# Quarter sums moved from GpSimd to VectorE, seven products added up in PSUM on copied seeds, first gate group left whole

## The chip, the cores and the metric

One core of one Trainium2 chip runs the whole program. The metric is the device time of one execution in microseconds (us). The kernel before takes 1243.79 us, the median of three runs (1243.25 to 1244.95).

Engines are named as the profile names them: PE is TensorE (PEld its weight loads), DVE is VectorE, ACT is ScalarE, POOL is GpSimd, SP is SyncE, which issues nearly all DMAs.

## The reference

Two transformer blocks follow each other on 512 tokens of width 1024, all in float32. The change touches the second block's feed-forward part alone:

```python
D_FF = -(-8 * D_MODEL // (3 * 256)) * 256          # 2816
h = rmsnorm_2(x, ffn_norm_g[l])
x = x + (jax.nn.silu(h @ w_gate[l]) * (h @ w_up[l])) @ w_down[l]
return rmsnorm_2(x, final_norm_g)
```

Here h is 512 x 1024 and w_gate and w_up are 1024 x 2816.

## The kernel before

Each float32 operand of a matmul is split in two float32r parts, high (`hi`, `wh`) and low (`lo`, `wl`), and each product is three matmuls: high by high, high by low, low by high. For a weight tile, ACT casts the high part (line 257) and DVE subtracts it to get the low part (line 258). Four weight tiles (`wh`, `wl`) are held at a time; `used` (L261) frees one when PE has finished it, and converts the next one that fits.

**Gate and up in seven products.** Columns of w_gate and w_up are taken in 12 groups (`quartered`): group 0 is gate columns 0 to 511, group 1 is up columns 0 to 511, and so on; groups 10 and 11 are 256 wide. A group's weight is cut into four quarters (A11, A21, A12, A22: two halves of the 1024 rows by two halves of the columns), and so is h (B11, B21, B12, B22: two halves of the width by two halves of the tokens). With the sums S1 to S4 of weight quarters and T1 to T4 of quarters of h, seven quarter products replace eight (the Winograd form of Strassen's scheme). `SEVEN` (L158) names, for each product, the operand of h, the PSUM bank R1 to R4 that it goes to, and whether it starts that bank afresh (`True`) or adds to what is there.

Each quarter product of a full group is 24 matmuls (2 column blocks x 4 row blocks x 3) of 128 x 128 weights and 256 tokens; a group is 168 of them, groups 10 and 11 are 84 each, together 1848.

**Who does what.** `Quarters.load` (L172) brings a quarter in by DMA (512 KB) into a ring of six places; `Quarters.add` (L185) forms S1 to S4 on POOL, tile name `qsum`, in one of three places. `quarters_T` (L210), called for each block `tb` of 128 tokens, transposes the normalized activations on PE (L1214), copies them to `h3f`, splits B11 and B21 for the first two blocks, and for the last two forms T1 to T4 on POOL (L1223 to L1229, tile `tsum`), each split on ACT and DVE as soon as it is there. `Sevenfold.run` (L1293) issues the matmuls (L1301) and combines: after A11, ACT copies R1 to SBUF as p1; DVE forms u2 = p1 + R2, u3 = p1 + R2 (a second R2), and the three result quarters c22, c21, c12 (L1290); C11 is read from R1. `out` (L1273) applies silu to gate groups (tile `ag`) or multiplies up groups by it (tile `fa`).

**Order.** The list `seven` sets the order of products: A11 and A12 of groups 0 and 1 first, which need only the first 256 tokens, then the other five products of group 0, those of group 1, and from group 2 on the order of `SEVEN`. PE runs inside `ordered()` in the order written. The other engines' queues are laid out by a scheduler; each engine takes its queue strictly in order. Before this stage PE runs the out-projection's second half, `product("o21", ...)`, whose evacuation `ev_o2` (L1233) gives the normalized tokens; behind it comes the down projection (`dn0`, `dn1`, matmuls on L342), whose activations `fs` are split by `place` (L1346).

## Time and profile before

| | before |
|---|---|
| median of 3 runs | 1243.79 us |
| profiled execution: time | 1242.61 us |
| profiled execution: span | 1240.9 us |
| mean granted TensorE clock | 0.993 |
| PE, DVE, ACT, POOL busy | 96%, 70%, 49%, 24% |
| gate/up stage (first to last L1301 matmul) | 859.49 to 1110.95 us |

The time holds 1.7 us outside the span. A PE row's duration is the latency of one pipelined matmul (a 256-column one lasts 0.28 us), so PE's busy sum says little on how tight its work is packed; how far apart matmuls start, and the waits put down to PE, say more. DVE, ACT and POOL rows start a little before the one ahead of them has ended, so a queue's pace is read from start to start.

### The profile page before, as it was taken

What the parts mean: (1) busy time and instruction counts of PE and PEld (TensorE: products, weight loads), DVE (VectorE), ACT (ScalarE), POOL (GpSimd) and SP (SyncE); (2) the same over time, 40 slices, a digit from 0 to 9 for tenths busy, and PEclk for the clock granted to TensorE, in tenths of its full rate; (3) what the DMA queues carried; (4) which work ended last, traced back from release to release, by engine and by line L of the source; (5) the groups of instructions that cost most, each with busy time, mean ns of one, the idle gap of its engine ahead of it and who ended that gap; (6) DMA issues with size and microseconds to landing.
All of it is one profiled execution on the core that took longest, in us unless ns stands there. A gap on an engine that the chain in (4) does not pass through costs nothing.

```text
span 1240.9 us, 18922 instructions
## 1 busy us (share of the span) xinstructions
PE 1190.3 (96%) x6852; PEld 1031.4 (83%) x6852; DVE 868.6 (70%) x1779; ACT 603.9 (49%) x1259; POOL 296.0 (24%) x363
## 2 busy tenths in 40 slices
PE   6999999999999999899999999998699999999997
PEld 5898788888888888699888898786699999988885
DVE  5678767896677455875555788765999999985322
ACT  4565456545653344444566677535334434463212
POOL 2011033101210023402111122103855555410201
PEclk9999999999999999999999999999899999999999
DMA  5412311321123432334221312452233333244321
GB/s 188 106 58 68 121 33 53 109 83 51 52 89 119 170 119 86 119 91 112 69 68 53 88 37 68 137 170 85 67 103 104 102 112 93 69 152 122 100 86 68
DMA packets 79804, 117.19 MB, mean 94 GB/s; under 512 B 10336, under 2 KB 43360, under 8 KB 79712
## 3 DMA queue, kind: packets, MB, share of 16 engines
q1 hardware_dynamic: 79712, 115.99, 29.9%
q8 instruction: 54, 0.88, 0.3%
q14 instruction: 38, 0.31, 0.1%
HBM read 109.68 MB, written 6.29 MB: 93 GB/s over the span
## 4 chain that ended last, share of the span: by engine, by line
PE 81%; DVE 10%; issue 3%; ACT 2%; POOL 2%; DMA 1%; SPq 0%; POOLq 0%; DVEq 0%; ACTq 0%
PE mm L342 55%; PE mm L1301 11%; PE R L1301 4%; DVE wl L258 3%; PE AV L589 3%; PE T L574 2%; DVE acts L442 1%; ACT wh L257 1%; PE S L807 1%; PE S L808 1%; PE T L473 1%; DMA raw<-in_w_in_dram 1%; PE T L1100 1%; POOL var L458 0%; POOL eg L973 0%
## 5 line engine op out<-in xcount | busy, mean ns | idle before, releaser
L258 DVE TENSOR_TENSOR wl<-raw,wh 128x512 fp32r<-128x512 f32 (+6 forms) x199 | 181.2, 930 | 137.7 <-ACT wh L257 136.9
L257 ACT CAST wh<-raw 128x512 fp32r<-128x512 f32 (+6 forms) x199 | 153.9, 799 | 191.0 <-PE mm L342 126.8
L534 POOL TENSOR_SCALAR P<-P,rr 128x256 f32<-128x256 f32 (+3 forms) x128 | 69.1, 540 | 310.3 <-DVE rr L532 216.2
L1301 PE MATMUL mm<-acts,wh 128*128 128x256 f32 x704 | 128.6, 284 | 8.5 <-DVE u L1290 5.3
L1301 PEld LDWEIGHTS mm<-acts,wh 128*128 128x128 f32 x704 | 109.1, 190 | 10.3 <-issue 10.1
L342 PE MATMUL mm<-wh,fs 128*128 128x512 f32 x352 | 110.5, 395 | 0.2 <-ACT fs L444 0.2
L342 PE MATMUL mm<-hh,wh 128*128 128x512 f32 x256 | 103.6, 405 | 0.0
L342 PE MATMUL mm<-hl,wh 128*128 128x512 f32 x256 | 101.4, 396 | 0.0
L342 PE MATMUL mm<-hh,wl 128*128 128x512 f32 x256 | 100.3, 395 | 0.0
L1301 PE MATMUL mm<-acts,wl 128*128 128x256 f32 x352 | 99.4, 283 | 0.0
L442 DVE TENSOR_TENSOR pl<-T,ph 128x128 fp32r<-128x128 f32 (+3 forms) x152 | 62.3, 411 | 30.6 <-ACT ph L441 30.0
L258 DVE TENSOR_TENSOR wl<-qsum,wh 128x1024 fp32r<-128x1024 f32 (+1 forms) x48 | 81.0, 1687 | 2.6 <-ACT wh L257 2.3
L257 ACT CAST wh<-qsum 128x1024 fp32r<-128x1024 f32 (+1 forms) x48 | 46.9, 977 | 68.4 <-PE mm L1301 43.5
L342 PEld LDWEIGHTS mm<-wh,fs 128*128 128x128 f32 x352 | 65.9, 188 | 16.5 <-ACT fs L444 0.4
L1301 PE MATMUL R<-acts,wh 128*128 128x256 f32 x352 | 66.6, 289 | 13.4 <-ACT p L1307 13.4
L441 ACT CAST ph<-T 128x128 fp32r<-128x128 f32 (+3 forms) x152 | 55.1, 363 | 49.7 <-PE T L574 36.9
L192 POOL TENSOR_TENSOR qsum<-quart 128x1024 f32<-128x1024 f32 (+1 forms) x24 | 57.6, 2398 | 84.9 <-DMA quart<-in_w_gate_dram 53.6
L526 ACT ACTIVATE P<-P,nm 128x128 f32<-128x128 f32 (+2 forms) x96 | 51.5, 536 | 47.2 <-DVE nm L519 43.7
L342 PE MATMUL mm<-wl,fs 128*128 128x512 f32 x176 | 69.7, 397 | 0.4 <-DVE wl L258 0.4
L258 DVE TENSOR_TENSOR wl<-quart,wh 128x1024 fp32r<-128x1024 f32 (+1 forms) x36 | 65.6, 1828 | 4.1 <-ACT wh L257 4.1
L1301 PEld LDWEIGHTS R<-acts,wh 128*128 128x128 f32 x352 | 56.4, 196 | 13.9 <-ACT p L1307 13.8
L1301 PEld LDWEIGHTS mm<-acts,wl 128*128 128x128 f32 x352 | 67.0, 190 | 0.0
(376 smaller groups left out, 3259.6 us busy)
## 6 DMA issues: line engine op xcount, KB each, us to landing
raw<-in_w_in_dram SPq DMA_DIRECT2D x50, 512.0 KB, 3.6
raw<-in_w_down_dram SPq DMA_DIRECT2D x22, 512.0 KB, 3.7
quart<-in_w_gate_dram SPq DMA_DIRECT2D x20, 512.0 KB, 3.9
quart<-in_w_up_dram SPq DMA_DIRECT2D x20, 512.0 KB, 3.9
raw<-in_w_merge_dram SPq DMA_DIRECT2D x16, 512.0 KB, 3.6
raw<-in_w_out_dram SPq DMA_DIRECT2D x16, 512.0 KB, 3.7
raw<-in_w_ple_gate_dram SPq DMA_DIRECT2D x8, 512.0 KB, 3.7
raw<-in_w_branch_b_dram SPq DMA_DIRECT2D x4, 512.0 KB, 3.5
```

The lines of the kernel that those rows point to most:

```text
L192: nc.gpsimd.tensor_tensor(t, self.parts[a], self.parts[b], op=op)
L257: nc.scalar.copy(hi[:, js], raw[:, js])
L258: mark[0] = nc.vector.tensor_sub(lo[:, js], raw[:, js], hi[:, js].bitcast(F32)).ins
L342: nc.tensor.matmul(o, x_, m, start=kc == 0 and k == 0 and n0 == 0, stop=last and k == 2)
L441: nc.scalar.copy(hi, src)
L442: nc.vector.tensor_sub(lo, src, hi.bitcast(F32))
L473: nc.tensor.transpose(T[:, i, :], src[:, blk(c + i)], ident)
L526: nc.scalar.activation(P[:, :n], P[:, :n], AF.Exp, bias=bias, scale=-1.0, accum_out=rs)
L534: nc.gpsimd.tensor_scalar(P[:, :n], P[:, :n], rr, 1.0, op0=OP.mult, op1=OP.mult)
L574: nc.tensor.transpose(T[:, i, :], P[:, blk(i)], ident)
L589: nc.tensor.matmul(self.av[:, q0:q0 + pc.stop - pc.start], self.v(kb), m, start=pi == 0 and i == 0, stop=pi == len(plan) - 1 and i == 1)
L1301: nc.tensor.matmul(R[:, c, :], w[:, kc, cs], m[:, kc, :], start=first and c + kc + k == 0, stop=kc == 3 and k == 2, skip_group_check=True)
```

## The change

Six things change. (1) S1 to S4 are formed on DVE, not on POOL. (2) T1 to T4 are formed on DVE, most of them later, in `quarter_sums`, called when the first gate columns are evacuated; T4 changes its sign. (3) Group 0 is no quartered group any more: `fg0` is a plain product of 512 columns by 8 row blocks, in the order "half" (first the first 256 tokens of all four column blocks, then the last 256): 192 matmuls of 256 tokens instead of 168. It needs B12 split too, and takes four 512 KB weight tiles as `raw`. (4) u2 and u3 are added up by PE: ACT copies R1 into R2's bank, on which S2 and S3 add, and then R2 into R4's bank, on which A22 adds; ACT also copies R3 (p5) and R2 (u2) to SBUF. (5) R3 moves from an `mm` bank to one of the transposes' banks (E). (6) The order of products becomes A11(1), then for each group S1, S2, A12, S3, the next group's A11, A22, S4.

```diff
     }
 
 
-    SEVEN = {"A11": ("B11", 1, True), "S1": ("T1", 3, True), "S2": ("T2", 2, True), "A12": ("B21", 1, False),
-             "S3": ("T3", 2, False), "A22": ("T4", 4, True), "S4": ("B22", 3, False)}
+    SEVEN = {"A11": ("B11", 1, True), "S1": ("T1", 3, True), "S2": ("T2", 2, False), "A12": ("B21", 1, False),
+             "S3": ("T3", 2, False), "A22": ("T4", 4, False), "S4": ("B22", 3, False)}
     ring, sums = {}, []
 
     class Quarters:
...
             t = self.parts[name] = self.view(sums[i])
             a, op, b = {"S1": ("A21", OP.add, "A22"), "S2": ("S1", OP.subtract, "A11"),
                         "S3": ("A11", OP.subtract, "A21"), "S4": ("A12", OP.subtract, "S2")}[name]
-            nc.gpsimd.tensor_tensor(t, self.parts[a], self.parts[b], op=op)
+            nc.vector.tensor_tensor(t, self.parts[a], self.parts[b], op=op)
 
         def load_for(self, name):
             for q in {"S1": ("A21", "A22"), "A11": ("A11",), "A12": ("A12",)}.get(name, ()):
...
                 self.add(name)
             return self.parts[name]
 
+    specs["fg0"] = ([(w_gate_2, 0, 512, 0)], 8)
     specs_tail = {f"dn{i}": ([(w_down_2, 512 * i, 512, 0)], 22) for i in range(2)}
     quartered = []
     for i in range(6):
         for w in (w_gate_2, w_up_2):
             quartered.append(Quarters(w, 512 * i, 512 if i < 5 else 256))
-    early = ("A11", "A12")
-    seven = [(g, name) for g in (0, 1) for name in early]
-    seven += [(g, name) for g in (0, 1) for name in SEVEN if name not in early]
-    seven += [(g, name) for g in range(2, 12) for name in SEVEN]
+
+    seven = [(1, "A11")]
+    for g in range(1, 12):
+        seven += [(g, name) for name in ("S1", "S2", "A12", "S3")]
+        seven += [(g + 1, "A11")] if g < 11 else []
+        seven += [(g, name) for name in ("A22", "S4")]
 
     stream, first_of = [], {}
 
...
             else:
                 names, tag = {"B11": (("B11", "B21"), "U0"), "B21": (("B11", "B21"), "U0"),
                               "T3": (("T3", "B22"), "U1"), "B22": (("T3", "B22"), "U1"),
-                              "T1": (("T1", "T2"), "U6"), "T2": (("T1", "T2"), "U6")}[name]
-                t = unit("acts", tag, [128, 4, 4, 256])
+                              "T1": (("T1", "T2"), "U6"), "T2": (("T1", "T2"), "U6"),
+                              "B12": (("B12",), "U4")}[name]
+                t = unit("acts", tag, [128, 2 * len(names), 4, 256])
                 for i, n in enumerate(names):
                     acts[n] = [t[:, 2 * i], t[:, 2 * i + 1]]
         return acts[name]
...
             return
         b11, b21 = [h3f[:, c:c + 4, blk(tb - 2)] for c in (0, 4)]
         b12, b22 = [h3f[:, c:c + 4, blk(tb)] for c in (0, 4)]
-        t1, t2, t3, t4 = [p2("tsum", [128, 4, 128]) for _ in range(4)]
-        nc.gpsimd.tensor_sub(t1, b12, b11)
-        act_split("T1", tb, t1)
-        nc.gpsimd.tensor_sub(t2, b22, t1)
-        act_split("T2", tb, t2)
-        nc.gpsimd.tensor_sub(t3, b22, b12)
-        act_split("T3", tb, t3)
-        nc.gpsimd.tensor_sub(t4, t2, b21)
-        act_split("T4", tb, t4)
+        act_split("B12", tb, b12)
         act_split("B22", tb, b22)
+        sums_T.append((tb, b11, b12, b21, b22))
+
+    sums_T = []
+
+    def quarter_sums():
+
+        t12 = {}
+        for tb, b11, b12, b21, b22 in sums_T:
+            t12[tb] = [p2("tsum", [128, 4, 128]) for _ in range(2)]
+            nc.vector.tensor_sub(t12[tb][0], b12, b11)
+            act_split("T1", tb, t12[tb][0])
+            nc.vector.tensor_sub(t12[tb][1], b22, t12[tb][0])
+            act_split("T2", tb, t12[tb][1])
+        for tb, b11, b12, b21, b22 in sums_T:
+            t3, t4 = [p2("tsum", [128, 4, 128]) for _ in range(2)]
+            nc.vector.tensor_sub(t3, b22, b12)
+            act_split("T3", tb, t3)
+            nc.vector.tensor_sub(t4, b21, t12[tb][1])
+            act_split("T4", tb, t4)
 
     def ev_o2(nh):
         def f(tb, ps):
...
 
         def bank(self, i):
             if i not in self.R:
-                b = s_bank("R") if i == 1 else mm_bank()
+                b = s_bank("R") if i == 1 else t_bank("E").rearrange("p a b -> p (a b)") if i == 3 else mm_bank()
                 self.R[i] = b[:, :256 * self.n].rearrange("p (c t) -> p c t", c=self.n)
             return self.R[i]
 
...
                 ft, at = fa_at(4 * (self.g // 2) + c)
                 nc.vector.tensor_mul(ft[:, at:at + n, tok], v, gates[half][:, :n, tok])
 
-        def plus(self, name, a, b, op=OP.add):
-            t = self.sb(name)
-            nc.vector.tensor_tensor(t, a, b, op=op)
-            return t
-
         def run(self, name, hi, lo):
             b, i, first = SEVEN[name]
             bh, bl = act_pair(b)
...
                         nc.tensor.matmul(R[:, c, :], w[:, kc, cs], m[:, kc, :], start=first and c + kc + k == 0,
                                          stop=kc == 3 and k == 2, skip_group_check=True)
                     yield 0.5
-            s, R = self.s, self.R
+            R = self.R
             if name == "A11":
-                s["p1"] = self.sb("p1")
-                nc.scalar.copy(s["p1"], R[1])
+                nc.scalar.copy(self.bank(2), R[1])
+            elif name == "S1":
+                self.p5 = self.sb("p5")
+                nc.scalar.copy(self.p5, R[3])
             elif name == "S2":
-                s["u2"] = self.plus("u2", s["p1"], R[2])
+                self.u2 = self.sb("u2")
+                nc.scalar.copy(self.u2, R[2])
             elif name == "A12":
                 self.out(0, 0, R[1])
             elif name == "S3":
-                s["u3"] = self.plus("u3", s["p1"], R[2])
-                self.out(1, 1, self.plus("c22", s["u3"], R[3]))
+                nc.scalar.copy(self.bank(4), R[2])
+                c22 = self.sb("c22")
+                nc.vector.tensor_add(c22, R[2], self.p5)
+                self.out(1, 1, c22)
             elif name == "A22":
-                self.out(1, 0, self.plus("c21", s["u3"], R[4], OP.subtract))
+                self.out(1, 0, R[4])
             elif name == "S4":
-                self.out(0, 1, self.plus("c12", s["u2"], R[3]))
+                c12 = self.sb("c12")
+                nc.vector.tensor_add(c12, R[3], self.u2)
+                self.out(0, 1, c12)
 
     def sevenfold():
         groups = {}
...
             if g not in groups:
                 groups[g] = Sevenfold(g)
             if name == "S1" and g % 2 == 0:
-                gates.clear() if g else None
+                gates.clear()
             convert_to(i)
             for c in groups[g].run(name, *ws[i]):
                 yield c
                 tick(c)
             used(i)
 
+    class Halves:
+
+
+        def __init__(self, *halves):
+            self.halves = halves
+
+        def __getitem__(self, key):
+            return self.halves[key[1].start // 256][key[0], key[1].start % 256:(key[1].stop - 1) % 256 + 1]
+
+    def act_halves(kc):
+        h, k = divmod(kc, 4)
+        return [Halves(*[act_pair(f"B{h + 1}{t}")[i][:, k, :] for t in (1, 2)]) for i in range(2)]
+
+    def ev_g(c, ps):
+        if not gates:
+            gates.update({i: pool.tile([128, 2, 512], F32, name="ag", tag=f"V{2 + i}") for i in range(2)})
+            quarter_sums()
+        silu_gate(gates[c // 2][:, c % 2, :], ps)
+
     with ordered():
-        for _ in itertools.chain(product("o21", pair_act(yh, yl), ev_o2(1), True, "all"), sevenfold()):
+        for _ in itertools.chain(product("o21", pair_act(yh, yl), ev_o2(1), True, "all"),
+                                 product("fg0", act_halves, ev_g, False, "half"), sevenfold()):
             pass
 
     ssf = pool.tile([128, NB, 2], F32, name="ssf", tag="ssf")
```

**DVE at the start of the stage.** Before, from the evacuation of the last token block (`x_8945<-x_8945,mm` is its residual sum) on; `wl<-quart` are low parts of quarters, `acts` low parts of B and T:

```order
L1236 TENSOR_TENSOR x_8945<-x_8945,mm 128x512
L258 TENSOR_TENSOR wl<-quart,wh 128x1024 x3
L442 TENSOR_TENSOR acts<-tsum,acts 128x4x128
L1243 SCALAR_TENSOR_TENSOR xn<-x_8945,rstd,gb 128x1024
L258 TENSOR_TENSOR wl<-qsum,wh 128x1024
L442 TENSOR_TENSOR acts<-h3f,acts 128x4x128
L442 TENSOR_TENSOR acts<-tsum,acts 128x4x128 x2
L442 TENSOR_TENSOR t_9314<-tsum,t_9313 128x4x128
```

After, the same place; `wl<-raw` are the low parts of fg0's weight tiles 1 to 3, `tsum` T sums, `qsum` S sums:

```order
L1251 TENSOR_TENSOR x_8945<-x_8945,mm 128x512
L261 TENSOR_TENSOR wl<-raw,wh 128x1024
L1237 TENSOR_TENSOR tsum<-h3f 128x512
L1239 TENSOR_TENSOR tsum<-h3f,tsum 128x512
L1258 SCALAR_TENSOR_TENSOR xn<-x_8945,rstd,gb 128x1024
L445 TENSOR_TENSOR acts<-h3f,acts 128x4x128
L261 TENSOR_TENSOR wl<-raw,wh 128x1024
L192 TENSOR_TENSOR qsum<-qsum,quart 128x1024
L445 TENSOR_TENSOR acts<-tsum,acts 128x4x128
L445 TENSOR_TENSOR acts<-h3f,acts 128x4x128
L445 TENSOR_TENSOR acts<-tsum,acts 128x4x128
L261 TENSOR_TENSOR wl<-raw,wh 128x1024
```

DVE now forms four sums here itself, and fg0's tiles 2 and 3 (the last two `wl<-raw`) stand behind them.

**DVE over one full up group.** Before, group 3: `u` and `c` are the sums on L1290:

```order
L1290 TENSOR_TENSOR u_10124<-p_10063,mm 128x512
L258 TENSOR_TENSOR wl<-qsum,wh 128x1024
L1286 TENSOR_TENSOR fa<-R,ag 128x2x256
L258 TENSOR_TENSOR wl<-quart,wh 128x1024
L1290 TENSOR_TENSOR u_10187<-p_10063,mm 128x512
L1290 TENSOR_TENSOR c_10189<-u_10187,mm 128x512
L258 TENSOR_TENSOR wl<-qsum,wh 128x1024
L1286 TENSOR_TENSOR fa<-c_10189,ag 128x2x256
L1290 TENSOR_TENSOR c_10222<-u_10187,mm 128x512
L258 TENSOR_TENSOR wl<-qsum,wh 128x1024
L1286 TENSOR_TENSOR fa<-c_10222,ag 128x2x256
L1290 TENSOR_TENSOR c_10255<-u_10124,mm 128x512
```

After, group 3 (`c` are c22 and c12, E is R3's bank):

```order
L1301 TENSOR_TENSOR fa<-R,ag 128x2x256
L261 TENSOR_TENSOR wl<-qsum,wh 128x1024
L192 TENSOR_TENSOR qsum<-quart 128x1024
L261 TENSOR_TENSOR wl<-qsum,wh 128x1024
L1328 TENSOR_TENSOR c_10191<-mm,p_10097 128x512
L192 TENSOR_TENSOR qsum<-quart,qsum 128x1024
L1301 TENSOR_TENSOR fa<-c_10191,ag 128x2x256
L261 TENSOR_TENSOR wl<-qsum,wh 128x1024
L1301 TENSOR_TENSOR fa<-mm,ag 128x2x256
L192 TENSOR_TENSOR qsum<-quart 128x1024
L261 TENSOR_TENSOR wl<-quart,wh 128x1024
L1334 TENSOR_TENSOR c_10285<-E,u_10127 128x512
```

Per group two u sums and c21 have gone, and four `qsum` have come, each some products ahead of its use.

**ACT over one full up group.** Before, group 3, from p1's copy (`p_10063<-R`) to the next group's:

```order
L1307 COPY p_10063<-R 128x512
L257 CAST wh<-quart 128x1024
L257 CAST wh<-qsum 128x1024
L257 CAST wh<-quart 128x1024
L257 CAST wh<-qsum 128x1024 x2
L257 CAST wh<-quart 128x1024
L257 CAST wh<-qsum 128x1024
L1307 COPY p_10287<-R 128x512
```

After, group 3: `p` is R3's copy p5, `u` is u2, `mm<-mm` the seed of R4, `mm<-R` the seed of R2 for the next group:

```order
L1319 COPY p_10097<-E 128x512
L260 CAST wh<-quart 128x1024
L1322 COPY u_10127<-mm 128x512
L260 CAST wh<-qsum 128x1024 x2
L1326 COPY mm<-mm 128x512
L260 CAST wh<-qsum 128x1024
L1316 COPY mm<-R 128x512
L260 CAST wh<-quart 128x1024
```

Between the casts of weights (7 a group, as before) stand four copies out of PSUM instead of one.

## Rows read from the trace of the kernel before

**Rows 1.** Page: busy us (share), instructions by engine.

```profile
PE 1190.3 (96%) x6852; PEld 1031.4 (83%) x6852; DVE 868.6 (70%) x1779; ACT 603.9 (49%) x1259; POOL 296.0 (24%) x363
```

**Rows 2.** Windows: us; busy of PE, PEld, DVE, ACT, POOL; PEclk, DMA.

```profile
859.49:915.00 55.51, 38.35 (x281) 37.35 (x279) 53.57 (x37) 25.39 (x35) 41.54 (x19) 0.88 0.25 76
915.00:1080.00 165.00, 160.92 (x1349) 159.86 (x1349) 158.85 (x130) 71.02 (x81) 87.26 (x33) 1.00 0.32 96
1080.00:1110.95 30.95, 29.54 (x242) 28.63 (x241) 26.21 (x44) 16.36 (x30) 7.33 (x6) 1.00 0.42 142
1110.95:1240.90 129.95, 122.41 (x526) 98.11 (x524) 45.37 (x53) 36.70 (x54) 11.25 (x16) 0.98 0.30 96
```

**Rows 3.** Waits of PE, 850 to 1115 us: total, times, longest.

```profile
PE R L1301 <- ACT p L1307: 13.4, 2, 8.6
PE mm L1301 <- DVE u L1290: 5.3, 2, 2.9
```

**Rows 4.** PE in time: start, us, instruction, [idle before <-releaser].

```profile
868.59 0.80 PE L1301 MATMUL R<-acts,wh 128*128 128x256 f32 x2 [4.82 <-ACT p L1307]
...
885.26 0.79 PE L1301 MATMUL R<-acts,wh 128*128 128x256 f32 x2 [8.56 <-ACT p L1307]
...
898.34 0.48 PE L1301 MATMUL mm<-acts,wh 128*128 128x256 f32 x2 [2.89 <-DVE u L1290]
```

**Rows 5.** Chain that ended last, in time: start, us, what.

```profile
1006.55 2.84 PE R L1301 x24
1009.39 5.69 PE mm L1301 x48
...
1018.93 3.27 DVE wl L258
```

**Rows 6.** DVE groups by shape, 915 to 1080 us: busy, mean ns, idle.

```profile
L258 DVE TENSOR_TENSOR wl<-qsum,wh 128x1024 fp32r<-128x1024 f32 x33 | 61.2, 1855 | 2.0 <-ACT wh L257 1.9
L258 DVE TENSOR_TENSOR wl<-quart,wh 128x1024 fp32r<-128x1024 f32 x24 | 50.3, 2098 | 2.2 <-ACT wh L257 2.2
```

**Rows 7.** POOL groups by shape, 915 to 1080 us.

```profile
L192 POOL TENSOR_TENSOR qsum<-quart 128x1024 f32<-128x1024 f32 x15 | 38.5, 2570 | 19.5 <-DVE wl L258 19.5
```

**Rows 8.** DVE in time, around the start of the stage.

```profile
860.49 0.68 DVE L1236 TENSOR_TENSOR x<-x,mm 128x512 f32<-128x512 f32 x1
...
896.39 1.22 DVE L258 TENSOR_TENSOR wl<-qsum,wh 128x1024 fp32r<-128x1024 f32 x1
897.52 0.68 DVE L1290 TENSOR_TENSOR u<-p,mm 128x512 f32<-128x512 f32 x1
898.12 3.06 DVE L258 TENSOR_TENSOR wl<-qsum,wh 128x1024 fp32r<-128x1024 f32 x1
```

**Rows 9.** POOL in time, around the start of the stage.

```profile
864.68 1.41 POOL L451 TENSOR_TENSOR rstd<-var,mhalf 128x1 f32<-128x1 f32 x1
...
897.68 2.41 POOL L192 TENSOR_TENSOR qsum<-quart 128x1024 f32<-128x1024 f32 x1 [4.10 <-DVE wl L258]
```

**Rows 10.** DVE groups by shape, 1111 to 1150 us (POOL idle).

```profile
L258 DVE TENSOR_TENSOR wl<-raw,wh 128x1024 fp32r<-128x1024 f32 x9 | 11.0, 1222 | 13.7 <-ACT wh L257 13.7
L445 DVE SCALAR_TENSOR_TENSOR fs<-fa,fs 128x512 fp32r<-128x512 f32 x16 | 10.0, 682 | 0.0
```

**Rows 11.** ACT groups by shape, 915 to 1080 us.

```profile
L257 ACT CAST wh<-qsum 128x1024 fp32r<-128x1024 f32 x32 | 33.5, 1048 | 44.5 <-PE mm L1301 28.6 <-PE R L1301 7.3 <-issue 4.0
L1307 ACT COPY p<-R 128x512 f32<-128x512 f32 x8 | 4.6, 578 | 0.0
```

**Rows 12.** ACT in time: second h copy of block 2; first fs.

```profile
862.78 0.57 ACT L1215 COPY h3f<-T 128x512 f32<-128x512 f32 x1
...
1103.88 2.19 ACT L444 ACTIVATE fs<-fa 128x512 fp32r<-128x512 f32 x4
```

**Rows 13.** DMA issues, 855 to 1110 us: KB, median us to landing.

```profile
quart<-in_w_up_dram SPq DMA_DIRECT2D x18, 512.0 KB, 3.9
```

**Rows 14.** DMA issues, 785 to 800 us; the same columns.

```profile
quart<-in_w_up_dram SPq DMA_DIRECT2D x2, 512.0 KB, 6.3
```

## The prediction

> **What bounds the kernel now.** I read the page's busy shares first, then the stretches of the gate/up stage, PE's waits in it and what PE did in time there, and last the rows of DVE and POOL. PE is busy 96% of the span [rows 1], so only work taken from PE, or holes in its work, can move the time. The windows show where the holes are: the granted clock is 1.00 from 915 us to 1110.95 us, but 0.88 in the first 55.5 us of the stage, where PE's latencies overlap to only 38.35 us [rows 2].
>
> How tight PE could be is read from the chain: 72 matmuls in 2.84 + 5.69 = 8.53 us, 0.1185 us each at full clock [rows 5]. The stage has 1848 of them, 219.0 us, and lasts 251.5 us (859.49 to 1110.95). Transposes (16 of 128 columns) and 4 down-projection matmuls of 512 columns take about 2 us, an estimate by the same time per column. So some 30.5 us of the stage are loss:
> - Middle stretch: 165 - 1349 x 0.1185 = 5.1 us.
> - Last stretch: 30.95 less 238 x 0.1185 and 0.95 for the four down matmuls: 1.8 us.
> - First stretch: the rest, 23.6 us.
>
> In the first stretch three stalls of 4.82, 8.56 and 2.89 us [rows 4] make 16.3; the remainder is mostly the clock (12% of 55.5 us is 6.7). The profile puts the two long ones on ACT's copy of p1, once 8.6 us, and the third on a u sum of DVE [rows 3]. Those are last links only: the queues in front of them are full of T and S sums on POOL and of DVE subtractions that run slowly beside them.
>
> That slowness is the second thing to see. A low-part subtraction of 128x1024 takes 1.22 us when POOL is idle [rows 10] and the same one 3.06 us while POOL adds from 897.68 on [rows 8, 9]; over the middle stretch its mean is 1.86 and 2.10 us [rows 6]. DVE is thereby busy 158.85 of 165 us [rows 2]: it sets the pace of the middle, by a little. In the chain a slow wl of 3.27 us stands where PE's products end [rows 5].
>
> **The change part by part.** *Sums leave POOL.* A POOL sum lasts 2.57 us in the mean [rows 7], and costs DVE more than DVE's own sum would: each subtraction that it overlaps loses 1 to 2 us. In start-to-start time a DVE instruction takes 1.13 us for 1024 elements and 0.60 for 512 (starts at 896.39, 897.52, 898.12) [rows 8]. A full group after: 7 low parts and 4 sums, 11 x 1.13 = 12.4 us; 2 combining sums and 4 outputs, 6 x 0.60 = 3.6; together 16.0 us. PE needs 168 x 0.1185 = 19.9 us a group. DVE before needs 20 us of its 20.6 us a group (158.85 of 165). So PE becomes the bound, with 3.9 us a group to spare on DVE. A DVE sum of two 1024-element SBUF tiles is not in the trace; its neighbours are the subtraction alone, 1.22, and beside POOL, up to 3.06 [rows 8, 10]. I take 1.22, since no POOL work is left beside it; the upper end is the slow rival. POOL's rstd, 1.41 us behind a T sum [rows 9], also gets shorter, and the last block's normalized rows come earlier.
>
> Here a rule of the Trainium skill speaks against the change. "Perfetto Trace Analysis", section "Optimizing Scalar/DVE Operations", advises moving work off a saturated DVE, to ScalarE or even GpSimd; this does the reverse, on a DVE at 96% of its stretch. By that half the sum would be that of the slow rival below. The same passage warns that the two engines share a read port, so that moving work between them may not help; by this half DVE's load falls, as I take it. The durations with and without POOL bear out the second half.
>
> *In-order waits.* Each `qsum` is about one product ahead of need or more: S1 of a group stands on DVE before the low part of the previous group's A12, some nine products (25 us) before PE uses it. Its quarter lands in a median 3.9 us [rows 13], and its ring place frees with an S3 sum about two products (5.7 us) earlier. Held behind a late one would be the low parts, three products (8.5 us) ahead of PE. So I cost these waits at nothing; without that cover each would cost its lateness, once a group.
>
> *Seeds.* S2 waits for R2's copy, some three products ahead: hidden. Two copies have just one product's time, 2.84 us [rows 5]: u2 (R2 to SBUF) before S3, hidden by A12, and R2 to R4 before A22, hidden by the next A11. Ahead of each in ACT's queue is one cast. Cast 1.05 and copy 0.58 [rows 11], with some 0.1 of signalling, make 1.75 us: 1.1 us to spare. A copy from PSUM to PSUM is not in the trace; between 0.58 (PSUM to SBUF) and 1.05 (SBUF to SBUF, double the size) it stays hidden at both ends. The u3, c21 and one u sum that go lie off PE.
>
> So the middle loses 0 to 2 us instead of 5.1; I take 1: **4.1 gained**.
>
> *First group whole.* 24 matmuls more, 2.8 us. It needs no T and no S sum. Walking DVE's new queue from 860.49 [rows 8] at its paces: residual sum to 861.1, tile 1 to 862.2. PE, which reaches tile 1 at about 861.7, stalls 0.6. Then T1; T2 waits for block 2's second copy (862.78 + 0.57) [rows 12]: 864.0; normalized rows 865.2; one half split 865.8; tile 2 866.9; an S sum 868.1; three splits 869.9; tile 3 871.0. PE has by then done 56 matmuls and both transposes, at about 868.8: a stall of 2.2 us, with two ends: none if the scheduled sums run quicker than this, and 4.8 us, the first stall of before [rows 4], if a weight tile's DMA is late. Tile 3's DMA can be issued when tile 1 is converted, 862.3, and lands by 866.2 [rows 13]; its cast is done at 867.5: hidden by DVE. After the stall the clock takes something: I take 1.0 us, between 0 and the 6.7 us that three stalls had. The second half of fg0's tokens, 40 matmuls later at 877, wants B12 and B22 of the last block, split by 874: hidden. Weight tiles come free only in fg0's last 2 us, so A11(1) is cast and split in the 2.3 us around its end, which I cost at nothing (0 to 1). The later T sums end near 881, before S1 needs them at 891.
>
> First stretch: 2.8 + 0.6 + 2.2 + 1.0 = 6.6 instead of 23.6: **17.0 gained**.
>
> *Last groups.* ACT's queue puts eight `fs` (2.19 us for four) [rows 12] and two casts ahead of the seed for the last A22, some 5.6 us behind A12(11); PE fills it with S3 (1.4 us) and 14 down matmuls (3.3): a hole of 1.0 against 1.8 before. **0.8 gained**, between -2 and 1.8.
>
> *Earlier.* One S sum now stands in DVE's queue among the last attention head's splits, and waits for a quarter that takes up to 6.3 us to land beside three others [rows 14]. I take **0.5 lost** (0 to 1.1).
>
> Sum: 4.1 + 17.0 + 0.8 - 0.5 = 21.4 us. The profiled execution took 1242.61 us (span 1240.9 and 1.7 around it); it would take 1221.2. The median of the runs is 1.2 us above it: **1222 us**.
>
> **The rivals.**
> 1. *DVE's order gives half back.* PE's slack of three low parts is eaten by a sum that waits for its quarter, or a seed comes late, about 1 us a group over ten groups: 1232 us. For: DVE and ACT are strictly in order, and two seeds have only 1.1 us to spare. Against: DVE has 3.9 us a group left, and landing has 1.8 us of cover at worst.
> 2. *The start is smooth.* No stall at tile 3 and no clock loss: 3 us better, and nothing lost in the middle: 1218 us or a little under. For: DVE's walk adds whole paces one after another. Against: tile 3 stands behind eight other instructions.
> 3. *DVE stays slow and becomes the bound.* If the wide instructions kept the middle's mean of 1.9 us without POOL, 11 x 1.9 + 3.6 = 24.5 us a group instead of 20.6, ten times: 39 slower, 18 gained at the ends: 1265 us. It decides from about (20.6 + 1.8 - 3.6) / 11 = 1.7 us per wide instruction. For: 1.9 is the mean that this stage shows. Against: in stretches without POOL every one is at 1.22 [rows 10].
> 4. *Nothing happens:* late loads or clock eat the start's gain and the middle stays as it is, 1243 us. Nothing in the profile asks for it.
>
> **How the numbers follow.** The forecast has 0.67, with a range of its own of 1217 to 1228 (stall 0 to 4.8, middle 0 to 2, ends as given). Rival 1 has 0.17, rival 2 0.10, rival 3 0.04, rival 4 0.02. The range 1214 to 1232 leaves out the slower half of rival 1, rival 3 and rival 4. Within 0.2% (2.5 us) is about what a measurement of this kernel can't tell from no change: 0.02. Slower: 0.04. Faster: 0.94.
>
> **What would show it.** Right: wide DVE instructions of the stage at 1.22 us and DVE near 80% busy in it; two groups in 39.8 us instead of 41; only one stall over 1 us before the first quartered product, at fg0's tile 3, on a DVE wl; the seed copies under 0.7 us and no PE wait put down to them but the last. Wrong: PE waits on ACT copies or on `qsum` once a group, DVE at 95%, or a granted clock under 0.95 over the stage's first 50 us. A time above 1232 us or below 1214 us would mean that a mechanism is missing here.

## The result, and the profile after

| | before | after |
|---|---|---|
| median of the runs beside each other | 1243.52 us (1243.14 to 1244.95, 4 runs) | 1223.53 us (1222.66 to 1225.47, 4 runs) |
| profiled execution: time, span | 1242.61, 1240.9 us | 1223.95, 1222.2 us |
| ratio of the times | | 0.9839, 95% interval 0.9822 to 0.9856 |
| stage, first gate/up matmul to last | 859.49 to 1110.95 us | 860.67 to 1094.5 us |

The forecast was 1222 us, the range 1214 to 1232. The stage's windows after, to be laid beside [rows 2] (us; busy time of PE, PEld, DVE, ACT, POOL; granted clock; DMA share and GB/s):

```profile
859.49:915.00 55.51, 52.66 (x423) 51.68 (x422) 48.20 (x57) 30.09 (x43) 0.74 (x2) 0.97 0.35 106
915.00:1080.00 165.00, 165.00 (x1400) 165.00 (x1399) 134.94 (x150) 86.06 (x117) 0.00 (x0) 1.00 0.30 93
```

PE latencies now cover the whole middle stretch, where they left 4.08 of 165 us open before. DVE is busy 82% of it, not 96%. In the first stretch the clock is 0.97 where it was 0.88, and 423 instructions of PE are recorded there, not 281.

The stalls that are left are two at the start and two at the end. PE in time (start, us, instruction, [idle before <-releaser]):

```profile
863.54 0.38 PE L345 MATMUL mm<-acts,wl 128*128 128x256 f32 x1 [0.49 <-DVE wl L261]
...
872.60 0.58 PE L345 MATMUL mm<-acts,wl 128*128 128x256 f32 x1 [2.22 <-DVE wl L261]
...
1087.56 0.74 PE L345 MATMUL mm<-wh,fs 128*128 128x512 f32 x2 [1.58 <-ACT fs L447]
1088.62 0.74 PE L345 MATMUL mm<-wl,fs 128*128 128x512 f32 x2 [0.33 <-DVE wl L261]
```

They take the place of [rows 4]. The first two stand where the prediction put them, at fg0's tiles 1 and 3 (0.6 and 2.2 foreseen). Between 873 and 1087 us PE is never seen to wait. Note the 0.58 us of the matmul behind the longer stall, against 0.38 behind the short one: the clock has fallen, and narrow windows behind the stall show for how long (from 876.60 to 878.60 us it is 1.00 again):

```profile
872.60:874.60 2.00, 2.00 (x9) 2.00 (x10) 2.00 (x3) 0.28 (x1) 0.00 (x0) 0.50 0.41 83
874.60:876.60 2.00, 2.00 (x14) 2.00 (x13) 2.00 (x4) 0.81 (x2) 0.00 (x0) 0.71 0.93 294
```

0.50 is the lower level (1.2 GHz). The chain of waits gives the price (start, us, what):

```profile
872.60 17.77 PE mm L345 x136
...
910.37 5.66 PE E L1311 x48
...
950.01 5.66 PE E L1311 x48
```

At the pace of [rows 5] the 136 matmuls would take 16.1 us, so 1.65 us are lost to the clock. The two rows behind it are the same two products, two groups apart: 950.01 - 910.37 = 39.64 us for two groups.

Two prices that were only bounded before are now rows of the groups by shape, 915 to 1080 us. First DVE, then ACT (busy, mean ns, idle):

```profile
L261 DVE TENSOR_TENSOR wl<-qsum,wh 128x1024 fp32r<-128x1024 f32 x30 | 36.7, 1224 | 10.9 <-ACT wh L260 10.9
...
L192 DVE TENSOR_TENSOR qsum<-quart 128x1024 f32<-128x1024 f32 x13 | 15.9, 1220 | 0.1
```

```profile
L1326 ACT COPY mm<-mm 128x512 f32<-128x512 f32 x8 | 4.6, 578 | 0.0
L1319 ACT COPY p<-E 128x512 f32<-128x512 f32 x8 | 4.6, 578 | 0.0
```

The low part is back at 1.22 us (1.86 and 2.10 in [rows 6]), DVE's own sum of two SBUF tiles costs the same 1.22, as taken, and a copy from PSUM to PSUM, the seed, 0.58 us, just what the copy to SBUF costs.

### The profile page after: what moved, and what is told of

Same layout as the page of the kernel before. It is cut to its first block, busy times and chain, and to the rows that moved or that the text cites. A ratio compares the mean times of both kernels' runs of the same rounds, so it can differ in the third digit from the quotient of the medians.

```text
span 1222.2 us, 18908 instructions
## 1 busy us (share of the span) xinstructions
PE 1188.5 (97%) x6876; PEld 1030.8 (84%) x6876; DVE 821.8 (67%) x1792; ACT 615.0 (50%) x1290; POOL 157.5 (13%) x307
## 4 chain that ended last, share of the span: by engine, by line
PE 84%; DVE 6%; issue 3%; POOL 2%; ACT 2%; DMA 2%; SPq 0%; POOLq 0%; ACTq 0%; DVEq 0%
PE mm L345 57%; PE mm L1311 7%; PE R L1311 5%; PE E L1311 5%; PE AV L592 3%; PE T L577 3%; DVE wl L261 1%; PE S L810 1%; PE S L811 1%; PE T L476 1%; ACT wh L260 1%; DMA raw<-in_w_in_dram 1%; PE T L1103 1%; DMA quart<-in_w_up_dram 1%; POOL var L461 1%
## 5 line engine op out<-in xcount | busy, mean ns | idle before, releaser
L261 DVE TENSOR_TENSOR wl<-raw,wh 128x512 fp32r<-128x512 f32 (+6 forms) x203 | 186.1, 936 | 139.6 <-ACT wh L260 138.5
L261 DVE TENSOR_TENSOR wl<-qsum,wh 128x1024 fp32r<-128x1024 f32 (+1 forms) x44 | 49.5, 1126 | 13.4 <-ACT wh L260 13.4
L1311 PE MATMUL R<-acts,wh 128*128 128x256 f32 x320 | 57.8, 281 | 0.0
L1311 PE MATMUL mm<-acts,wh 128*128 128x256 f32 x320 | 57.6, 280 | 0.0
L345 PEld LDWEIGHTS mm<-hh,wl 128*128 128x128 f32 x256 | 48.0, 188 | 11.2
L1311 PE MATMUL E<-acts,wh 128*128 128x256 f32 x320 | 57.1, 280 | 0.0
L577 PE MATMUL T<-ident,P 128*128 128x128 f32 x296 | 54.5, 277 | 2.4 <-DVE km L445 1.2
L345 PEld LDWEIGHTS mm<-hh,wh 128*128 128x128 f32 x256 | 48.2, 188 | 8.5
L345 PEld LDWEIGHTS mm<-hl,wh 128*128 128x128 f32 x256 | 48.2, 188 | 7.8
L345 PE MATMUL mm<-h2h,wh 128*128 128x512 f32 x128 | 53.4, 417 | 0.0
```

What stands on the lines that cost most here:

```text
L261: mark[0] = nc.vector.tensor_sub(lo[:, js], raw[:, js], hi[:, js].bitcast(F32)).ins
L345: nc.tensor.matmul(o, x_, m, start=kc == 0 and k == 0 and n0 == 0, stop=last and k == 2)
L577: nc.tensor.transpose(T[:, i, :], P[:, blk(i)], ident)
L1311: nc.tensor.matmul(R[:, c, :], w[:, kc, cs], m[:, kc, :], start=first and c + kc + k == 0, stop=kc == 3 and k == 2, skip_group_check=True)
```

## The experiments

Each is described by its edit against the kernel before or the kernel after. All times are medians; two kernels that were not run beside each other are compared by their ratios to the kernel before, which was run beside each. Diffs are cut; `...` marks what is left out.

**The sums alone, on the kernel before (`b_sums_dve`).**

```diff
-            nc.gpsimd.tensor_tensor(t, self.parts[a], self.parts[b], op=op)
+            nc.vector.tensor_tensor(t, self.parts[a], self.parts[b], op=op)
...
-        nc.gpsimd.tensor_sub(t1, b12, b11)
+        nc.vector.tensor_sub(t1, b12, b11)
...
```

The other three T sums move in the same way.

> The kernel before with only its S and T sums moved from GpSimd to VectorE; group 0 stays quartered, the sums u and c stay on VectorE. My theory is that two separate things gave the 20 us: the end of contention in the middle (4 us), and a first group that waits for no T and no S sum (16 us). By it this kernel gets the middle's part, wide VectorE instructions near 1.22 us and VectorE at 17.8 of 19.9 us a full group, while the start keeps a stall of 5 to 9 us before group 0's S1 on the T1 of the last token block, which is formed in the same crowded queue: about 1232 us (1229 to 1236). Rival: the contention alone was the harm, in the start as well, and sums on VectorE end all stalls: 1225 us or less. Second rival: VectorE becomes the bound without the seeds: 1243 us or more.

Measured: 1232.71 us, ratio 0.9901 (0.9888 to 0.9915). The middle is closed, the start is not. Its windows, and its stalls in time:

```profile
859.00:915.00 56.00, 43.57 (x322) 42.37 (x322) 50.62 (x60) 27.67 (x38) 2.81 (x2) 0.88 0.31 96
915.00:1080.00 165.00, 165.00 (x1398) 165.00 (x1397) 150.66 (x171) 72.98 (x83) 0.00 (x0) 1.00 0.32 93
```

```profile
871.40 0.80 PE L1301 MATMUL R<-acts,wh 128*128 128x256 f32 x2 [6.94 <-ACT p L1307]
...
883.75 0.80 PE L1301 MATMUL R<-acts,wh 128*128 128x256 f32 x2 [3.08 <-ACT p L1307]
```

So the sums' move is worth the middle's 5 us and 5 to 7 of the start (12 us in all by the ratio, 10.4 between the two profiled spans). In the start, stalls of 6.94 and 3.08 us on the same copy are left of 4.82 and 8.56 [rows 4]. Without the whole first group the rest stays.

**The whole first group taken back, on the kernel after (`a_g0_quartered`).**

```diff
-    specs["fg0"] = ([(w_gate_2, 0, 512, 0)], 8)
...
-    seven = [(1, "A11")]
+    seven = [(g, name) for g in (0, 1) for name in ("A11", "A12")]
+    seven += [(0, name) for name in ("S1", "S2", "S3", "A22", "S4")]
+    seven += [(1, "S1"), (1, "S2"), (1, "S3"), (2, "A11"), (1, "A22"), (1, "S4")]
...
```

B12 is not split, and the T sums are formed as soon as the last token block is there.

> The kernel after with group 0 taken in seven quarter products again, its A11 and A12 and those of group 1 first; sums stay on VectorE, seeds stay in PSUM. My theory (the whole first group buys time until the T sums are there): a stall of 5 to 9 us before group 0's S1, some 1 to 2 us more at seeds, 2.8 us of matmuls saved: about 1230 us (1227 to 1234). Rival (the sums' move did it all): no such stall, and the 24 matmuls saved: 1221 us.

Measured: 1231.59 us, ratio 0.9889 (0.9876 to 0.9903): 8 us more than the kernel after by the medians and 6 by the ratios, in the theory's range, though PE has 2.8 us less to do. The stall before S1 is shorter than I wrote (2.25 us, on T1's low part); ACT's copies stall more, 8.4 us in five waits. All the stalls of its first 55 us:

```profile
867.05 0.50 PE L1313 MATMUL R<-acts,wh 128*128 128x256 f32 x2 [2.08 <-ACT mm L1318]
875.72 0.50 PE L1313 MATMUL R<-acts,wh 128*128 128x256 f32 x2 [1.85 <-ACT mm L1318]
882.72 0.39 PE L1313 MATMUL E<-acts,wh 128*128 128x256 f32 x1 [2.25 <-DVE acts L446]
891.59 0.50 PE L1313 MATMUL mm<-acts,wh 128*128 128x256 f32 x2 [1.50 <-ACT u L1324]
896.19 0.50 PE L1313 MATMUL mm<-t,wh 128*128 128x256 f32 x2 [1.51 <-ACT mm L1328]
909.31 0.50 PE L1313 MATMUL mm<-acts,wh 128*128 128x256 f32 x2 [1.50 <-ACT u L1324]
```

The size was right, and its parts were half wrong. In this order of products A12 follows A11, S3 follows S2 and (in group 0) A22 follows S3 directly, so no product covers the copy in between, and PE waits for the whole of it. The first two waits have a crowded ACT queue ahead of the copy. The other three, 1.50 us each, are just one cast and the copy. This is the wait that ends at 891.59 us, on ACT:

```profile
890.00 1.05 ACT L261 CAST wh<-qsum 128x1024 fp32r<-128x1024 f32 x1 [1.18 <-PE mm L1313]
890.96 0.58 ACT L1324 COPY u<-mm 128x512 f32<-128x512 f32 x1
```

The prediction reckoned 1.75 us for such a copy and hid it behind a product; here no product hides it. So this run doesn't tell the whole first group from the order that it allows: with group 0 whole, no quartered product has to run before the T sums are there, and each copy keeps its product of cover.

**The seeds taken out, on the kernel after (`a_no_seed`).** u2, u3 and c21 are added on DVE from a copy of R1 in SBUF, as before.

```diff
-                nc.scalar.copy(self.bank(2), R[1])
+                self.p1 = self.sb("p1")
+                nc.scalar.copy(self.p1, R[1])
...
-                nc.scalar.copy(self.u2, R[2])
+                nc.vector.tensor_add(self.u2, R[2], self.p1)
...
```

> The kernel after with u2, u3 and c21 added on VectorE from a copy of R1 in SBUF, as before, so that no bank is seeded. VectorE then needs 17.8 instead of 16.0 us a full group of PE's 19.9. My theory (PE is the bound once GpSimd is out, with slack on VectorE): no change, 1223.5 us (1222 to 1225). Rival (the seeds carry part of the gain, as VectorE's order delays low parts when its load rises): 1227 us or more, with waits of PE on wl in the middle stretch. Second rival: the last groups, where the seed for A22 stood in ACT's queue behind activations (1.6 us), get quicker without it: 1222 us.

Measured: 1220.54 us (1220.32 to 1222.07), ratio 0.9806 (0.9792 to 0.9819). None of the three: faster than any of them by a little, and nearest to the second rival. The middle is unchanged (PE busy 165.00 us of 165, its 1398 matmuls recorded against 1400; DVE busy 148.53). The end is what moved:

```profile
1080.00:1112.00 32.00, 32.00 (x179) 27.62 (x179) 28.02 (x48) 21.90 (x36) 0.00 (x0) 1.00 0.61 208
```

The profiled spans differ by 1.9 us (1220.3 and 1222.2), as much as the two stalls at 1087 us of the kernel after. Its ACT queue in time shows where they are from:

```profile
1083.85 2.19 ACT L447 ACTIVATE fs<-fa 128x512 fp32r<-128x512 f32 x4
1085.94 1.03 ACT L260 CAST wh<-raw 128x1024 fp32r<-128x1024 f32 x1
1086.88 2.19 ACT L447 ACTIVATE fs<-fa 128x512 fp32r<-128x512 f32 x4
1088.97 1.04 ACT L260 CAST wh<-raw 128x1024 fp32r<-128x1024 f32 x1
1089.91 0.37 ACT L1326 COPY mm<-mm 128x256 f32<-128x256 f32 x1
```

The last seed (1089.91) stands behind all that, S3 is done at 1086.0, and so PE's order has 14 down matmuls ahead of the last A22, which want the fs activations at once. Without the seed A22 and S4 follow S3 with no gap, and the activations have that time.

**The S sums back on GpSimd, on the kernel after (`a_sums_pool`).**

```diff
-            nc.vector.tensor_tensor(t, self.parts[a], self.parts[b], op=op)
+            nc.gpsimd.tensor_tensor(t, self.parts[a], self.parts[b], op=op)
```

> The kernel after with only the S sums formed on GpSimd again (T sums stay on VectorE). GpSimd's adds then overlap VectorE's subtractions: four sums of 2.57 us, half of a group's time. My theory by load: VectorE has 7 low parts at 1.2 to 2.1 us and 6 small ones, 12 to 18.3 us a group of PE's 19.9, so that even the slowed VectorE just keeps up, and the middle loses 0 to 2 us: 1222 to 1226 us; the stall at the whole group's fourth weight tile gets shorter by one sum (1.2 us). Rival (moving the S sums is what ended the middle's loss of 5 us): 1227 to 1230 us, with waits of PE on wl or qsum once a group.

Measured: 1223.15 us, ratio 0.9827 (0.9813 to 0.9840): no change, in the theory's range. The stall at the fourth weight tile shrank to 1.09 us as expected, but one of 1.67 us came at the third. The low parts are as slow as ever, but PE does not notice:

```profile
L261 DVE TENSOR_TENSOR wl<-quart,wh 128x1024 fp32r<-128x1024 f32 x23 | 58.8, 2580 | 0.0
L261 DVE TENSOR_TENSOR wl<-qsum,wh 128x1024 fp32r<-128x1024 f32 x30 | 57.5, 1920 | 0.7 <-ACT wh L260 0.6
```

```profile
915.00:1080.00 165.00, 165.00 (x1401) 165.00 (x1400) 159.44 (x117) 86.13 (x118) 84.96 (x36) 1.00 0.31 93
```

DVE is busy 159.44 us here and was 158.85 before [rows 2], at which PE lost 5 us. So DVE's busy share did not set the middle's pace, though the prediction says that it did.

**The kernel after once more (`after_again`),** run beside `n_sums_pool`, `a_sums_twice` and `n_hold`.

> The kernel after, unchanged, timed in the same call as the three below, since the gain that taking the seeds out gave (1220.54 us against 1223.53 us) comes from two calls. If chips differ, it reads otherwise here; I expect 1223.5 us (1222.5 to 1225.5).

Measured: 1224.26 us (1221.37 to 1224.50), ratio 0.9835 (0.9821 to 0.9848).

**Neither seeds nor sums on DVE (`n_sums_pool`).** These are the edits of the two experiments before, together. Of the change, the whole first group, the T sums, the order and the copy of R3 (p5, in its new bank) are left.

> The kernel after without seeds and with the S sums on GpSimd, so that of the change only the whole first group, the T sums and the order are left. With either the sums on VectorE (b_sums_dve, a_no_seed) or the seeds (a_sums_pool) the middle lost nothing, though VectorE was busy 159.4 of 165 us in the last of these. Theory: the middle's loss needs both burdens on VectorE at once, GpSimd beside it and the u and c sums on it, more than 20 us a group of PE's 19.9; it comes back here: PE waits of 3 to 8 us on c, u or wl between 915 and 1080 us, and 1224 to 1229 us. Rival: the middle's loss of before was left over from the crowded start, from which VectorE never caught up; with the whole first group it stays away: 1219 to 1221.5 us.

Measured: 1230.62 us, ratio 0.9896 (0.9883 to 0.9910), a little above the theory's range. The loss comes back, nearly twice as large as in the kernel before (165 - 1313 x 0.1185 = 9.4 us against 5.1). Its waits of PE in the middle, and the one row of its windows:

```profile
PE mm L1311 <- DVE u L1323: 6.4, 4, 2.4
```

```profile
915.00:1080.00 165.00, 158.63 (x1313) 157.93 (x1312) 155.84 (x132) 71.37 (x88) 79.07 (x32) 0.98 0.30 90
```

PE starts 85 matmuls fewer in it than in `a_no_seed` (1398): 85 x 0.1185 = 10.1 us, which is the whole of the difference to 1220.54 (8.4 us between the two profiled spans). DVE just ahead of the longest of these waits, then PE behind it:

```profile
939.10 3.41 DVE L261 TENSOR_TENSOR wl<-quart,wh 128x1024 fp32r<-128x1024 f32 x1
942.43 0.68 DVE L1323 TENSOR_TENSOR u<-mm,p 128x512 f32<-128x512 f32 x1
```

```profile
940.53 0.28 PE L1311 MATMUL R<-acts,wl 128*128 128x256 f32 x1
943.25 0.77 PE L1311 MATMUL mm<-acts,wh 128*128 128x256 f32 x2 [2.45 <-DVE u L1323]
```

This is the mechanism of the middle here. The sum u (u2) reads R2's bank after S2, and S3 adds to that bank, so u has the time of the one product between them, A12 (2.84 us). It takes 0.68 us itself; here it stands behind a low part held up by GpSimd, and PE waits. PE never waits for a low part in this stretch.

The kernel before has the same mechanism at two places. Its waits of PE from 915 to 1080 us, and the end of one of the three on c (DVE, then PE):

```profile
PE mm L1301 <- DVE u L1290: 2.5, 1, 2.5
PE mm L1301 <- DVE c L1290: 2.1, 3, 0.7
```

```profile
1022.71 0.68 DVE L1290 TENSOR_TENSOR u<-p,mm 128x512 f32<-128x512 f32 x1
1023.42 0.69 DVE L1290 TENSOR_TENSOR c<-u,mm 128x512 f32<-128x512 f32 x1
```

```profile
1024.26 0.48 PE L1301 MATMUL mm<-acts,wh 128*128 128x256 f32 x2 [0.68 <-DVE c L1290]
```

Here c22 reads R3, to which S4 adds, with only A22 between S3 and S4; u3 and c22 must both be done in that time, and ahead of them stands the low part of 3.27 us [rows 5]. In the kernel after and in `n_sums_pool` ACT copies R3 to SBUF (p5) right behind S1, so c22 holds up no product, and there is no wait on c. The two by two, all with the whole first group, the new order and p5:

| | sums on VectorE | S sums on GpSimd |
|---|---|---|
| **seeded** | 1223.53, 1224.26 (0.9839, 0.9835) | 1223.15 (0.9827) |
| **not seeded** | 1220.54 (0.9806) | 1230.62 (0.9896) |

Each of the two edits ends the middle's loss, and the second adds nothing to the first. With the old order only the sums' move was tried alone (`b_sums_dve`), and it suffices; whether seeds alone would do there is not shown.

**How near DVE is to its bound (`a_sums_twice`).** Each S sum is formed twice.

```diff
-            nc.vector.tensor_tensor(t, self.parts[a], self.parts[b], op=op)
+            for _ in range(2):
+                nc.vector.tensor_tensor(t, self.parts[a], self.parts[b], op=op)
```

> The kernel after with each S sum formed twice on VectorE, one right behind the other (the second result is the same). It puts the disputed load to the test: VectorE then needs 16.0 + 4 x 1.13 = 20.5 us a full group at its start-to-start pace, of PE's 19.9. My theory (VectorE's load decides, and its order costs nothing as long as there is slack): it is just over the bound, 0.6 us a group over ten groups and 2 us at the start, 1229 us (1226 to 1236). Rival (order: a doubled sum delays the low part behind it, which PE needs soon): 2.4 us a group and more, 1245 us or over. Second rival (pace has more slack than counted): 1225 us or less.

Measured: 1230.85 us, ratio 0.9899 (0.9884 to 0.9914), in the theory's range. DVE is full:

```profile
915.00:1080.00 165.00, 161.09 (x1353) 159.88 (x1353) 163.80 (x176) 81.13 (x108) 0.00 (x0) 1.00 0.31 91
```

4.5 us a group more on DVE cost 6.6 us in all (to 1224.26), not 45: the slack of 3.9 us a group that the prediction counted from start-to-start times is there. In the middle PE now waits for low parts, 3.9 us in four waits.

**Sums held behind the start's weight tiles, without seeds (`n_hold`).** In the kernel after three sums stand in DVE's queue ahead of the low part of fg0's tile 3 (two T sums and one S sum; the section on the change says four). Beside the edit of `a_no_seed`, DVE's queue here has group 1's S1 to S3 and all T sums only behind that low part.

```diff
...
+            load_to(first_of["seven"] + 4)
+            with tc.issue_after(mark[0]):
+                for n in ("S1", "S2", "S3"):
+                    quartered[1].add(n)
+                quarter_sums()
```

> The kernel after without seeds (a_no_seed, 1220.54 us), and with the first S sums of group 1 and the T sums held behind the fourth weight tile of the whole first group in VectorE's queue. My theory: the stall of 2.2 us at that tile is VectorE's queue alone, and the S sum that stood among the last attention head's splits cost about 1 us; both go, and the granted clock stays up: 1217 us (1216 to 1218.5). Rival: the tile's DMA or its cast is late as well, so that the stall moves to it: 1219 to 1220.5 us. Rival on the other side: the held sums now come too late for S1 of group 1: 1222 us or more, with a wait on acts or wl before it.

Measured: 1218.87 us (1217.84 to 1219.70), ratio 0.9798 (0.9784 to 0.9811) beside 0.9835 (0.9821 to 0.9848) of the kernel after: the fastest version found. In time it lies between theory and first rival; the trace shows both at work (PE in time, all stalls of the stage):

```profile
862.13 0.39 PE L345 MATMUL mm<-acts,wl 128*128 128x256 f32 x1 [0.48 <-DVE wl L261]
870.01 0.39 PE L345 MATMUL mm<-acts,wl 128*128 128x256 f32 x1 [0.67 <-DVE wl L261]
887.19 0.39 PE L1311 MATMUL R<-acts,wl 128*128 128x256 f32 x1 [0.46 <-DVE wl L261]
```

The 2.22 us are down to 0.67. What is left waits for the tile's cast, and the cast for the tile's DMA: ACT stands idle for 0.95 us before it starts the cast at 867.65 us. The clock stays at 1.00 in the first stretch. The intervals of `n_hold` and `a_no_seed` overlap (0.9784 to 0.9811, 0.9792 to 0.9819), so the 1.7 us between them are supported by the trace and not shown by the times.

**The seeds left out in the last group alone (`a_last_no_seed`).**

```diff
+            last = self.g == 11
+            first = first or last and name in ("S2", "A22")
...
-                nc.scalar.copy(self.bank(2), R[1])
+                self.p1 = self.sb("p1") if last else self.bank(2)
+                nc.scalar.copy(self.p1, R[1])
...
```

> The kernel after with the seeds left out in group 11 alone: there u2, u3 and c21 are added on VectorE, groups 1 to 10 keep their seeds. Theory: what the seeds cost (1223.5 to 1224.3 us with, 1220.5 without) lies in the last group only, where the copy of R2 into R4's bank stands behind eight fs activations on ScalarE, so that 14 down matmuls go ahead of the last A22 and wait 1.9 us for activations. Without the seed A22 follows S3 at once: 1221.5 us (1220 to 1222.5), and no wait between 1080 and 1095 us. Rival: the seeds cost something in every group, which no wait of TensorE shows: 1223 us or more.

Measured: 1222.69 us, but from 1219.12 to 1224.23, ratio 0.9823 (0.9806 to 0.9841): by time it tells nothing, as the interval holds both cases. Even ahead of the stage, which the edit does not touch, its profiled execution is 2.3 us quicker than that of the kernel after (the stage starts at 858.38 and 860.67 us). The trace does tell: no wait between 1080 and 1112 us, PE busy throughout.

```profile
1080.00:1112.00 32.00, 32.00 (x167) 27.01 (x166) 26.54 (x41) 20.68 (x33) 0.00 (x0) 1.00 0.55 179
```

That the hole of 1.9 us comes from group 11's seeds alone is thereby shown (the edit takes its u2 copy off ACT too); whether the seeds of the other groups cost the remaining one to two microseconds between 1224 and 1220.5 is not.

**Another order of places for the activations, with seeds, sums held (`a_hold_tail`).** The sums are held by the edit of `n_hold`.

```diff
...
-                    t = unit("fs", ("U0", "U6", "U1", "U5", "U2")[j // 4])
+                    t = unit("fs", ("U6", "U0", "U1", "U5", "U2")[j // 4])
```

> The kernel after with its seeds, with the first S sums and the T sums held behind the fourth weight tile of the whole first group (as in n_hold), and with the activations of the down projection put into another order of places, so that the place that comes free first takes the first four. Theory: both holes close, 2 us at each end and 1 us of the S sum that leaves the last attention head, as without seeds: 1219 us (1217.5 to 1220.5). Rival: the hole at the end is ScalarE's queue (two fs of 2.2 us, two casts of 1.0), whatever place comes free first, and only the start's part is gained: 1221 to 1222 us.

Measured: 1221.35 us, ratio 0.9814 (0.9800 to 0.9828): the rival. The hole stays, 1.05 us on a weight tile's cast and 0.86 on its low part:

```profile
1083.05 0.73 PE L345 MATMUL mm<-wh,fs 128*128 128x512 f32 x2 [1.05 <-ACT wh L260]
1084.64 0.51 PE L345 MATMUL mm<-wl,fs 128*128 128x512 f32 x1 [0.86 <-DVE wl L261]
```

Here the wait for activations is gone, and the cast behind them in ACT's queue is late instead.

## Why the prediction was right

It forecast 1222 us; 1223.53 was measured. Term by term, in the profiled executions:

*Middle, 4.1 gained: 5.1 measured.* The loss went from 5.1 us to nothing. Two groups take 39.64 us where 39.8 was foreseen. The reason given was half of it. GpSimd does hold up the low parts, and moving the sums does end that. But the prediction let DVE's busy share set the pace, and by that `a_sums_pool` (159.44 us busy) should lose as before. It lost nothing, and the step that fails is "it sets the pace of the middle, by a little". What PE waited for were short sums behind a held-up low part: u2 once (2.46 us) and u3 with c22 three times (2.1 us together). So "The u3, c21 and one u sum that go lie off PE" is wrong for u3. The seeds, which the prediction found "hidden" and credited with nothing, end the loss as well with the S sums still on GpSimd (shown with the new order alone), since u2 is then a copy on ACT and no longer in DVE's queue. A gain with two sufficient causes was put down to one; the sums' move alone gives it, so the number did not suffer.

*First group, 17.0 gained: about 14.9.* From 860.67 to the end of fg0, the added matmuls take 2.84 us, the stalls 0.49 and 2.22 (0.6 and 2.2 foreseen), the clock 1.65 (1.0 foreseen, between 0 and 6.7). By the prediction's way of counting, the stage of 233.8 us less 1872 matmuls, 16 transposes and 14 down matmuls at full pace leaves 7.7 us lost; less the last groups' 1.9 and with the added matmuls, the first group costs some 8.7 us where 6.6 were foreseen. The part that is in none of these terms, 1.5 us, lies in short gaps ahead of tile 3, around the transposes among others. `b_sums_dve` and `a_g0_quartered` show that neither the sums nor the whole group with its order does it alone: each without the other is 6 to 9 us slower than the kernel after.

*Last groups, 0.8 gained: 0.1 lost.* The hole was sized at 1.0 us and is 1.58 + 0.33 = 1.91, against 1.8 before. The order of ACT's queue and the 14 down matmuls that fill in were as described. The step that was mis-sized is that PE fills the time with S3 and 14 down matmuls: the second filling was not ready, since its own activations are in the same queue.

*Earlier, 0.5 lost: 1.0.* The S1 sum among the last attention head's splits makes PE wait once, in the kernel after:

```profile
798.54 0.38 PE L592 MATMUL AV<-pl,vm 128*128 128x256 f32 x1 [1.02 <-DVE pl L445]
```

That is within the bounds (0 to 1.1); it was 0.5 us in `after_again`, 0.8 in `a_no_seed` and 0.2 in `a_last_no_seed`, which have the same order. With the sum held the wait is gone.

Together 5.1 + 14.9 - 0.1 - 1.0 = 18.9 us, where the profiled executions differ by 18.7 and 21.4 were forecast. The rivals: the smooth start (1218) is what `n_hold` then made, at 1218.87. DVE as the bound needed 1.7 us a wide instruction, and they take 1.22; that it can be the bound `a_sums_twice` shows. A stalled seed once a group didn't happen in the kernel after, but copies do stall PE where the order of products leaves them uncovered (`a_g0_quartered`). Of the advice weighed from the Trainium skill ("Perfetto Trace Analysis", section "Optimizing Scalar/DVE Operations") the second half held: moving the sums alone from GpSimd to DVE (`b_sums_dve`) lowered DVE's busy time in the middle from 158.85 to 150.66 us; the rest, down to 134.94, is with the seeds.

## What to carry to other kernels

An engine's busy share doesn't tell whether it holds another up: with DVE at 159.44 of 165 us PE lost nothing, with 155.84 it lost 9 us. So find the instruction for which the other waits, and what stands ahead of it in its queue. Where several edits each end the same wait, undo them one by one and then together, or the gain is put down to the wrong one, and edits that cost something (here the seeds, 2 to 4 us) stay in. Work that fills a wait must not need the queue that causes it.

## What the runs showed of the hardware

*A sum on GpSimd stops a DVE instruction that reads two SBUF tiles; it does not slow it down.* In `n_sums_pool`, DVE and then GpSimd in time:

```profile
967.57 0.69 DVE L1328 TENSOR_TENSOR u<-mm,p 128x512 f32<-128x512 f32 x1
968.29 1.70 DVE L1330 TENSOR_TENSOR c<-u,p 128x512 f32<-128x512 f32 x1
...
971.70 3.38 DVE L261 TENSOR_TENSOR wl<-qsum,wh 128x1024 fp32r<-128x1024 f32 x1
```

```profile
967.04 2.40 POOL L192 TENSOR_TENSOR qsum<-quart 128x1024 f32<-128x1024 f32 x1 [2.63 <-DVE wl L261]
971.26 2.73 POOL L192 TENSOR_TENSOR qsum<-quart,qsum 128x1024 f32<-128x1024 f32 x1 [1.82 <-issue]
```

GpSimd's second sum ends at 973.99, and the low part that started 0.44 us behind it ends at 975.08, 1.09 later: it waited for the end and then took its own time. The same holds for the sum c (GpSimd ends at 969.44, c at 969.99). The sum u beside the same GpSimd instruction, with one operand in PSUM, takes its usual 0.69. The two instructions of [rows 8, 9] read likewise: 897.68 + 2.41 = 900.09, and the low part ends at 901.18. The Trainium skill says so in "SBUF — State Buffer", section "Summary: rules for kernel authors": if DVE has two SBUF inputs while GpSimd reads SBUF, the second to start is blocked until the first has ended. The section "Who interferes with whom" adds that a DVE instruction with at most one SBUF input (outside the 2-port modes) does not contend. These rows agree. So a sum given to GpSimd costs DVE up to 2.3 us (3.38 less 1.09), twice what DVE needs to form it itself.

*The clock behind a stall of PE.* In the kernel after, a stall of 2.22 us was followed by a granted clock of 0.50 for 2 us, 0.71 for the next 2, then 1.00. In `n_sums_pool` the two longest waits, 2.45 and 2.03 us, have the same mark: 0.50 and 0.72, and 0.64 and 0.51, in the two windows of 2 us behind each. So the 6.4 us of waits in its middle cost 9.4. Behind the 0.67 us of `n_hold` the clock stays at 1.00. The length of the stall does not decide it alone: in the kernel before, the wait of 2.46 us that ends at 916.71 is followed by 1.00 up to 945 us, and in `a_g0_quartered` the wait of 2.08 us is followed by 1.00 and the shorter one of 1.85 by 0.70 and 0.50. What decides is not shown here.
